# Turning the trunk by transposes of 64 rows instead of 128 in a two-layer hybrid decoder

## The chip, the cores and the metric

The kernel runs on one core of a Trainium2 chip. The metric is the device time in microseconds (us) of one execution, everything from the first load to the last store included. Times in this text are of the kernel before unless said otherwise.

Engines: PE multiplies matrices and transposes (PEld is its loading of weights, which overlaps), ScalarE (ACT), VectorE (DVE) and GpSimd (POOL) compute elementwise, SP issues the transfers. PE writes to PSUM, memory of 128 partitions in eight banks of 512 fp32 columns; ACT and DVE read it there.

## What is computed

Two layers of a decoder on 256 tokens of 1024 numbers, all in fp32. Cut to what matters here:

```python
def rms_norm(x, g):
    y = x * lax.rsqrt(jnp.mean(x * x, axis=-1, keepdims=True) + RMS_EPS)
    return y * g

def swiglu(x, w_gate, w_up, w_down):
    return (jax.nn.silu(x @ w_gate) * (x @ w_up)) @ w_down

h = x
for l in range(2):
    h = h + 0.5 * swiglu(rms_norm(h, ffn1_norm[l]), ...)      # 1024 -> 2816 -> 1024
    h = h + hybrid_mixer(rms_norm(h, mix_norm[l]), w_in[l], ...)  # three groups of attention heads
    h = h + 0.5 * swiglu(rms_norm(h, ffn2_norm[l]), ...)
```

So there are six stages (FFN, mixer, FFN in each layer), and at each of the five borders between them the trunk `h` has to be normed and turned, so that features lie on partitions for the matmuls that follow.

## The kernel before

**Precision.** A product in fp32 is made of three in a faster format: each operand is split into a high part (rounded) and a low part (the rest). A weight block of 128 x 1024 is loaded by SP, its high part `wh` is cast by ACT (L126) and its low part `wl` subtracted by DVE (L130). These splits run ahead of PE through the whole kernel, up to seven blocks.

**The trunk at a border.** `trunk` holds 256 tokens (two tiles `t` of 128 partitions) by 1024 features. The class `Norm` makes of it `xhl`: for each of eight blocks `m` of 128 features the turned 128 x 256 tokens, times the gain, as a high part (`high`, L364, on ACT) and a low part (`low`, L367, on DVE; it subtracts the high part from the product, and so reads both). Both read the turned block out of PSUM. The division by the root mean square comes later, out of sums of squares (`squares`, L390, on ACT; then L395, L350 on DVE).

**Halves.** A border is done in two halves of four blocks, `half(0)` and `half(1)`. `turn` (L370 to L376) puts the eight 128 x 128 transposes of a half into two banks of tag `acc`, two blocks `m` to a bank. Four high parts, four low parts and the squares follow.

**Where the halves stand.** Instructions stand on each engine in the order in which the code issues them; nothing reorders them. At the end of a FFN (`tail`, L659) the trunk is finished in four quarters `q` of 128 tokens x 512 features, each by 12 matmuls and a residual add on DVE (L419). `half(0)` stands behind quarter 2's residual, ahead of quarter 3's on DVE, while PE goes on with quarter 3's matmuls. `half(1)` needs the last residual; it stands in the next stage: in a mixer inside `index_queries` (L762) after the first two column groups of the first unit, in a FFN behind the first eight wide matmuls (L594). Behind a mixer the first half is taken apart: its transposes are `norm_T`, its parts `norm_out` (L1289 to L1300), which stands some matmuls later.

Of the ten halves, four are at the entry of the two mixers, four behind the two mixers, two between the layers. The border at the very start (`opening`) has transposes of its own and is not touched.

**After `half(1)` in a mixer.** DVE goes on with weight splits, the sum of squares and then L781, which takes the finished index queries out of the four `gu` banks. PE's next chunk of `w_in` goes into those banks.

**The helper that exists.** `turn(ps, i, src)` at module level (L177 to L180) transposes a block in two halves of 64 rows, one into each of two banks: out of rows 0 to 63 come 64 columns in the first bank, out of rows 64 to 127 in the second. Attention uses it already for its probabilities, keys and gates.

Of the kernel before, what the change touches and what calls it, by code (L numbers as in the profile page):

```python
# [10 lines left out]
F32 = mybir.dt.float32  # L11
F32R = mybir.dt.float32r
I32 = mybir.dt.int32
AF = mybir.ActivationFunctionType
ALU = mybir.AluOpType
# [3 lines left out]
P = 128  # L19
# [135 lines left out]
def kernel(ctx: ExitStack, tc: tile.TileContext, x, ffn1_norm, ffn1_w_gate, ffn1_w_up, ffn1_w_down,  # L155
# [16 lines left out]
    V, A, G, T = nc.vector, nc.scalar, nc.gpsimd, nc.tensor  # L172

    def bank(tag):
        return psum.tile([P, 512], F32, name="ps_" + tag, tag=tag)

    def turn(ps, i, src):  # L177
        for e, b in enumerate(ps):
            r = slice(64 * e, 64 * e + 64)
            T.transpose(b[:, 64 * i:64 * i + 64], src[r], ident[r, r])  # L180
# [21 lines left out]
    trunk = xp.tile([P, 2, D], F32, name="trunk")  # L202
    cst = cp.tile([P, 3 * P + 2 * LATE], F32, name="cst")
    ident = cp.tile([P, P], F32, name="ident")
    rows, more_rows = tmp(P)[:16], tmp(P)[:32]
    gT = cp.tile([P, 48], F32, name="gT")
# [33 lines left out]
    def add_ffn(wg, wu, wd, first=False):  # L240
# [24 lines left out]
        for f in range(NF):  # L265
            half("g", f)
            half("u", f)
            if f == NF - 1:
                half("d", f - 1 - DOWN_LAG)
            if DOWN_LAG <= f != NF - 2:  # L270
                half("d", f - DOWN_LAG)
# [82 lines left out]
    class Norm:  # L354
# [5 lines left out]
            self.h, self.l = self.x[:, :, 0], self.x[:, :, 1]  # L360
            self.ss = sm.tile([P, 4], F32, name="ss4", tag="ss4")

        def high(self, m, src):
            A.activation(self.h[:, m], src, AF.Copy, scale=gT[:, self.col + m:self.col + m + 1])  # L364

        def low(self, m, src):
            V.scalar_tensor_tensor(self.l[:, m], src, gT[:, self.col + m:self.col + m + 1],  # L367
                                   self.h[:, m].bitcast(F32), op0=ALU.mult, op1=ALU.subtract)

        def turn(self, mp):  # L370

            ps = bank("acc").rearrange("p (m s) -> p m s", m=2)
            for t in range(2):
                for i in range(2):
                    T.transpose(ps[:, i, t * P:(t + 1) * P], trunk[:, t, (2 * mp + i) * P:(2 * mp + i + 1) * P], ident)  # L375
            return ps  # L376

        def half(self, c):

            ps = [self.turn(2 * c + i) for i in range(2)]  # L380
            srcs = [(4 * c + i, ps[i // 2][:, i % 2]) for i in range(4)]
            for m, src in srcs:
                self.high(m, src)
            for m, src in srcs:
                self.low(m, src)
            for t in range(2):
                self.squares(t, c)

# [34 lines left out]
    def ffn(norm, nxt, aside=None, first=False):  # L423
# [86 lines left out]
        def opening():  # L510
# [5 lines left out]
            def split(i, m, high, E):  # L516

                src, h, l = low[i]
                ks = slice(2 * m, 2 * m + 2)
                high(h[:, ks], src[:, ks])  # L520
                E.tensor_tensor(l[:, ks], src[:, ks], h[:, ks].bitcast(F32), op=ALU.subtract)  # L521
# [24 lines left out]
            def squares(c):  # L546
                for t in range(2):
                    norm.squares(t, c)

            xT = turn(0)  # L550
            warm_up(BRIDGE)
            for m in range(2):
                ks = (2 * m, 2 * m + 1)
                parts(m, xT)
                split(0, m, G.tensor_copy, V)
                split(1, m, A.copy, G)
                for k in ks:
                    wide(0, k)
                if m:
                    xT = turn(2)  # L560
                for k in ks:
                    narrow(0, k)
                if m:
                    squares(0)
                    parts(2, xT)
                xT = turn(2 * m + 1)
                for k in ks:
                    wide(1, k)
                for k in ks:
                    narrow(1, k)  # L570
# [11 lines left out]
            for f, p in enumerate((p0, p1)):  # L582
                for w, u in zip(p.ws, high):
                    for part, v in zip(w, u):
                        part.extend(v[:, k, f * P:(f + 1) * P] for k in range(4))
# [104 lines left out]
    def mixer(l, norm, nxt):  # L690
# [113 lines left out]
        def post_ib(ps):  # L804
# [113 lines left out]
            def sums_in():  # L918
                low, high = (at.tile([P, 4, 2, P], F32, name="later" + k, tag=k) for k in ("kT", "later"))
                first = tab.rearrange("p a b t d -> p (a b t d)").rearrange("p (h c) -> p h c", c=P)  # L920
                st["later"], st["first"] = (low, high), first
                src = sums_of
                for dst, h, n in ((first, 0, P), (low, 0, S), (high, 4, S)):
                    to = dst.rearrange("p h b c -> p h (b c)") if n == S else dst
                    k = to.shape[1]
                    nc.sync.dma_start(to, bass.AP(tensor=src.tensor, offset=src.offset + h * S,
                                                    ap=[[0, P], [S, k], [1, n]]))
# [119 lines left out]
        def tanh():  # L1047
            ps, hr = st.pop("cg"), st["hr"]
            sg = at.tile([P, 2, 512], F32, name="sg", tag="sg")
            for t in range(2):  # L1050
                A.activation(sg[:, t], ps[t], AF.Tanh, scale=hr[:, t:t + 1])
            st["sg"] = sg
# [139 lines left out]
        def both_scores(_):  # L1192
            for fn in (scores, st["B"][0]):
                for p in range(2):
# [4 lines left out]
                    b=lambda p: st["B"][1](p), B=lambda p: st["B"][2](p), T=lambda _: tanh(), w=causal_part)  # L1199
# [11 lines left out]
        for name, cols in CHUNKS[1:]:  # L1211
            n = sum(c[1] for c in cols)
            ps = [bank("gu") for _ in range(2)]
# [18 lines left out]
        acc = [bank("acc") for _ in range(4)]  # L1232
        late_sb = xp.tile([P, 3, 4, S], F32, name="cT", tag="xhl")
        st["gate"] = late_sb[:, 2]
        after = {}
# [51 lines left out]
            after["norm"] = nxt()  # L1287

        def norm_T(_):  # L1289
            after["ps"] = [after["norm"].turn(i) for i in range(2)]  # L1290

        def norm_out(_):
            n, ps = after["norm"], after["ps"]
            for m in range(4):
                n.high(m, ps[m // 2][:, m % 2])
            for m in range(4):
                n.low(m, ps[m // 2][:, m % 2])
            for t in range(2):
                n.squares(t, 0)

        todo.update(f=lambda p: flip(p, acc[2:]), c=c_T, k=c_out, g=gate_T, l=gate_out, h=left, r=right, x=last_right,
                    p=lambda _: W.pump(), Z=residuals, N=norm_T, M=norm_out)
        do(AC_ORDER)
        W.pump()
# [3 lines left out]
    def before_mixer(l):  # L1308
        if l == 0:
            V.memset(causal[:, P:2 * P], 0.0)  # L1310
            for t in range(2):
                V.tensor_scalar(causal[:, 2 * t * P:(2 * t + 1) * P], future, NEG, None, op0=ALU.mult)
            V.tensor_tensor(gc[:, 0], gc[:, 0], gc[:, 1], op=ALU.mult)
            V.tensor_scalar(gc[:, 0], gc[:, 0], HD ** -0.5, None, op0=ALU.mult)
        mixer_tables(l)
# [8 lines left out]
    norm = Norm(0, 0)  # L1324
    turn_gains()
    for l in range(DEPTH):
        norm = ffn(norm, lambda: Norm(1, l), lambda: before_mixer(l), l == 0)
        norm = mixer(l, norm, lambda: Norm(2, l))
        norm = ffn(norm, (lambda: Norm(0, l + 1)) if l + 1 < DEPTH else None)
# [37 lines left out]
```

## Time and profile before

| | us |
|---|---|
| median of 3 runs | 1005.16 |
| lowest, highest | 1004.29, 1005.18 |
| the profiled execution | 1004.51 |
| its span from the first instruction to the last | 1002.8 |

| engine | busy, share of the span | instructions |
|---|---|---|
| PE | 100% | 5692 |
| DVE | 80% | 1484 |
| ACT | 60% | 1118 |
| POOL | 16% | 186 |

1.7 us of the profiled execution lie outside its span. In a timeline a row of "x8" is eight like instructions in a row: its start is that of the first, its duration reaches to the end of the last. Instructions of an engine overlap a little, so the next row can start before the one ahead has ended. What stands in brackets is the idle time of the engine before the row and what it waited for; an idle time is given only where the engine's last instruction had ended.

### The profile page before, as it was taken

The numbers are of one execution on the slowest core, as the hardware profiler recorded it, in microseconds if no ns is written. First come the engines' busy times: TensorE is split into PE (matmuls) and PEld (weight loads), VectorE is DVE, ScalarE is ACT, GpSimd is POOL, SyncE is SP. The second block draws the span as 40 slices with busy tenths as digits, with TensorE's granted clock in tenths as the row PEclk, the third lists the DMA queues.
The fourth block names the chain that finished last, engine by engine and source line by source line (L and its number), as shares of the span: only waits on it lengthen the run. The fifth ranks groups of instructions, "written<-read, shape, count | busy, mean of one in ns | idle before, by whom it ended". The sixth has DMA issues, their size and how long they took to land.

```text
span 1002.8 us, 15209 instructions
## 1 busy us (share of the span) xinstructions
PE 998.1 (100%) x5692; PEld 856.6 (85%) x5692; DVE 797.5 (80%) x1484; ACT 598.2 (60%) x1118; POOL 160.9 (16%) x186
## 2 busy tenths in 40 slices
PE   9999999999999999999999999999999999999998
PEld 8888888888878888888888888889888788888887
DVE  5977778789998777777888777787899877777776
ACT  6655555587776555555465555556868765555552
POOL 2002000057902000000000030001677110000000
PEclk9999999999999999999999999999999999999999
DMA  9865746475725555555655655565556255474731
GB/s 293 270 223 160 231 149 238 140 245 172 241 72 168 167 169 185 193 190 202 196 168 173 210 184 195 193 200 184 181 202 231 83 175 165 135 242 144 235 127 42
DMA packets 133498, 184.80 MB, mean 184 GB/s; under 512 B 7152, under 2 KB 106800, under 8 KB 133424
## 3 DMA queue, kind: packets, MB, share of 16 engines
q1 hardware_dynamic: 133392, 183.82, 56.1%
q8 instruction: 45, 0.74, 0.3%
q14 instruction: 29, 0.24, 0.1%
q10 hardware_dynamic: 32, 0.01, 0.0%
HBM read 182.75 MB, written 1.06 MB: 183 GB/s over the span
## 4 chain that ended last, share of the span: by engine, by line
PE 88%; DVE 9%; ACT 2%; issue 1%; POOL 0%; DVEq 0%; ACTq 0%; POOLq 0%
PE ps_gu L340 57%; PE ps_acc L340 29%; DVE wl L130 4%; DVE score L889 1%; PE ps_acc L375 1%; ACT p L1095 1%; DVE score L875 1%; DVE m L888 1%; DVE c_ss L728 0%; PE ps_acc L180 0%; PE ps_gu L180 0%; DVE tmp L1085 0%; DVE p L1113 0%; DVE xhl L367 0%; DVE amask L893 0%
## 5 line engine op out<-in xcount | busy, mean ns | idle before, releaser
L130 DVE TENSOR_TENSOR wl<-raw,wh 128x1024 fp32r<-128x1024 f32 (+2 forms) x342 | 418.6, 1232 | 28.8 <-ACT wh L126 28.8
L126 ACT CAST wh<-raw 128x1024 fp32r<-128x1024 f32 (+2 forms) x341 | 341.7, 1037 | 15.2 <-PE ps_acc L340 8.2
L340 PE MATMUL ps_gu<-xhl,wh 128*128 128x512 f32 (+1 forms) x1472 | 347.6, 388 | 0.0
L340 PEld LDWEIGHTS ps_gu<-xhl,wh 128*128 128x128 f32 x1472 | 272.6, 188 | 54.2 <-ACT wh L126 0.5
L340 PEld LDWEIGHTS ps_gu<-xhl,wl 128*128 128x128 f32 x1472 | 187.5, 191 | 4.1 <-DVE wl L521 0.2
L340 PE MATMUL ps_gu<-xhl,wl 128*128 128x256 f32 (+1 forms) x1472 | 190.3, 282 | 0.0
L484 DVE TENSOR_TENSOR tmp<-ps_gu,tmp 128x256 f32<-128x256 f32 x176 | 72.9, 423 | 109.6 <-ACT tmp L483 109.3
L340 PE MATMUL ps_acc<-wh,hh 128*128 128x512 f32 (+1 forms) x352 | 137.2, 390 | 0.0
L340 PE MATMUL ps_acc<-wl,hh 128*128 128x512 f32 (+1 forms) x352 | 137.1, 389 | 0.0
L340 PE MATMUL ps_acc<-wh,hl 128*128 128x512 f32 (+1 forms) x352 | 136.6, 388 | 0.0
L340 PE MATMUL ps_gu<-wh,xhl 128*128 128x512 f32 (+2 forms) x448 | 134.6, 376 | 0.1
L483 ACT COPY tmp<-ps_gu 128x256 f32<-128x256 f32 x176 | 63.5, 372 | 91.6 <-PE ps_gu L340 91.4
L498 ACT CAST hh<-tmp 128x256 fp32r<-128x256 f32 x80 | 32.6, 407 | 120.3 <-DVE tmp L495 120.3
L340 PEld LDWEIGHTS ps_gu<-wh,xhl 128*128 128x128 f32 x448 | 82.6, 188 | 14.7 <-issue 1.7
L490 ACT ACTIVATE tmp<-tmp 128x256 f32<-128x256 f32 x88 | 36.9, 419 | 83.3 <-DVE tmp L488 83.2
L340 PE MATMUL ps_gu<-wl,xhl 128*128 128x512 f32 (+2 forms) x224 | 83.2, 372 | 0.0
L340 PEld LDWEIGHTS ps_acc<-wh,hl 128*128 128x128 f32 x352 | 66.1, 188 | 13.8
L351 POOL TENSOR_TENSOR y_n<-msq,minus_half 128x2 f32<-128x2 f32 x6 | 7.0, 1175 | 440.2 <-DVE msq L350 440.2
L340 PEld LDWEIGHTS ps_acc<-wh,hh 128*128 128x128 f32 x352 | 66.3, 188 | 12.6
L340 PEld LDWEIGHTS ps_acc<-wl,hh 128*128 128x128 f32 x352 | 66.3, 188 | 12.4 <-DVE wl L130 0.2
L340 PEld LDWEIGHTS ps_gu<-wl,xhl 128*128 128x128 f32 x224 | 42.1, 188 | 5.7
L508 DVE TENSOR_TENSOR tmp<-tmp,rb 128x256 f32<-128x256 f32 x88 | 37.5, 427 | 3.0
(232 smaller groups left out, 902.4 us busy)
## 6 DMA issues: line engine op xcount, KB each, us to landing
raw<-in_ffn_w_down_dram SPq DMA_DIRECT2D x44, 1024.0 KB, 5.0
raw<-in_ffn_w_gate_dram SPq DMA_DIRECT2D x42, 1024.0 KB, 7.3
raw<-in_ffn_w_up_dram SPq DMA_DIRECT2D x42, 1024.0 KB, 8.1
raw<-in_w_in_dram SPq DMA_DIRECT2D x24, 1024.0 KB, 5.1
raw<-in_w_out_dram SPq DMA_DIRECT2D x8, 1024.0 KB, 5.0
raw<-in_w_in_dram SPq DMA_DIRECT2D x4, 768.0 KB, 4.6
raw<-in_w_in_dram SPq DMA_DIRECT2D x4, 656.0 KB, 4.1
raw<-in_ffn_w_gate_dram SPq DMA_DIRECT2D x3, 512.0 KB, 7.4
```

The lines of the kernel that those rows point to most:

```text
L126: self.nc.scalar.copy(hv, src)
L130: (engine or self.nc.vector).tensor_tensor(lv, self.srcs[self.n_low], hv.bitcast(F32), op=ALU.subtract)
L340: T.matmul(o, l, r, start=start, stop=stop, skip_group_check=True)
L375: T.transpose(ps[:, i, t * P:(t + 1) * P], trunk[:, t, (2 * mp + i) * P:(2 * mp + i + 1) * P], ident)
L483: A.copy(o, ps[:, 1])
L484: V.tensor_tensor(o, ps[:, 0], o, op=ALU.add)
L490: A.activation(th, t_, AF.Tanh, scale=0.5)
L498: (V.tensor_copy if late else A.copy)(hh, t_)
L508: V.tensor_tensor(t_, t_, norm.rb, op=ALU.mult)
L875: V.scalar_tensor_tensor(sc, rl[e][:, i * n:(i + 1) * n], st["iw"][:, t, h:h + 1], st["cmask"][t] if h == 0 else sc, op0=ALU.mult, op1=ALU ...
L888: V.max(out=m8, in_=st["score"][t])
L889: V.match_replace(out=st["score"][t], in_to_replace=m8, in_values=st["score"][t], imm_value=-3e38)
```

## The change

Each of the eight transposes of 128 rows in a half becomes two of 64 rows by the helper. All four blocks `m` of a half now lie in both banks: one bank holds the tokens that came from rows 0 to 63 of each tile (64 for each `t`), the other those from rows 64 to 127. The high and the low part of a block are each taken in two pieces of 128 columns, one out of each bank (`e` = 0 and 1), and written to two runs of 64 columns of `xhl`. The order in a half is: all transposes, all eight high pieces, all eight low pieces, the squares.

```diff
-        def high(self, m, src):
-            A.activation(self.h[:, m], src, AF.Copy, scale=gT[:, self.col + m:self.col + m + 1])
+        def place(self, x, m, e):
+            x = x[:, m]
+            return x if e is None else x.rearrange("p (t j) -> p t j", t=2)[..., 64 * e:64 * e + 64]
+
+        def high(self, m, src, e=None):
+            A.activation(self.place(self.h, m, e), src, AF.Copy, scale=gT[:, self.col + m:self.col + m + 1])
...
-            ps = bank("acc").rearrange("p (m s) -> p m s", m=2)
-            for t in range(2):
-                for i in range(2):
-                    T.transpose(ps[:, i, t * P:(t + 1) * P], trunk[:, t, (2 * mp + i) * P:(2 * mp + i + 1) * P], ident)
-            return ps
+        def turns(self, c):
+
+            ps = [bank("acc") for _ in range(2)]
+            for m in range(4):
+                for t in range(2):
+                    turn(ps, 2 * m + t, trunk[:, t, (4 * c + m) * P:(4 * c + m + 1) * P])
+            return [b.rearrange("p (m t j) -> p m t j", t=2, j=64) for b in ps]
+
+        def parts(self, c, ps):
+
+            for f in (self.high, self.low):
+                for m in range(4):
+                    for e in range(2):
+                        f(4 * c + m, ps[e][:, m], e)
 
         def half(self, c):
 
-            ps = [self.turn(2 * c + i) for i in range(2)]
-            srcs = [(4 * c + i, ps[i // 2][:, i % 2]) for i in range(4)]
-            for m, src in srcs:
-                self.high(m, src)
-            for m, src in srcs:
-                self.low(m, src)
+            self.parts(c, self.turns(c))
...
         def norm_T(_):
-            after["ps"] = [after["norm"].turn(i) for i in range(2)]
+            after["ps"] = after["norm"].turns(0)
```

Line numbers below `Norm` move by 4 to 6: L364 becomes L368, L367 L371, L419 L425, L781 L787.

On DVE at the entry of the first mixer there stand, before, three residuals, the four low parts of the first half, the last residual, a weight split and the four low parts of the second half. A name in brackets is the engine whose counter the instruction waits for:

```order
L419 SCALAR_TENSOR_TENSOR trunk<-ps_acc,trunk 128x512 [waits PE_49] x3
L367 SCALAR_TENSOR_TENSOR xhl<-ps_acc,gT,xhl 128x256 [waits PE_49,Activation_49]
L367 SCALAR_TENSOR_TENSOR xhl<-ps_acc,gT,xhl 128x256
L367 SCALAR_TENSOR_TENSOR xhl<-ps_acc,gT,xhl 128x256 [waits PE_49,Activation_49]
L367 SCALAR_TENSOR_TENSOR xhl<-ps_acc,gT,xhl 128x256
L419 SCALAR_TENSOR_TENSOR trunk<-ps_acc,trunk 128x512 [waits PE_49]
L130 TENSOR_TENSOR wl<-raw,wh 128x1024 [waits DMAHW1_49]
```

And on DVE at the same place after the change:

```order
L425 SCALAR_TENSOR_TENSOR trunk<-ps_acc,trunk 128x512 [waits PE_49] x3
L371 SCALAR_TENSOR_TENSOR xhl<-ps_acc,gT,xhl 128x2x64 [waits PE_49,Activation_49] x2
L371 SCALAR_TENSOR_TENSOR xhl<-ps_acc,gT,xhl 128x2x64 x6
L425 SCALAR_TENSOR_TENSOR trunk<-ps_acc,trunk 128x512 [waits PE_49]
L130 TENSOR_TENSOR wl<-raw,wh 128x1024 [waits DMAHW1_49]
```

There are eight low parts where there were four, and the two that wait for ACT are the first and the second: the first of each bank.

On PE, at the second half in the same mixer, before (`xhl` with `wh` are the index queries):

```order
L340 MATMUL ps_gu<-xhl,wl 128x192 x2
L375 MATMUL ps_acc<-ident,trunk 128x128 x2
L375 MATMUL ps_acc<-ident,trunk 128x128 [waits DVE_49]
L375 MATMUL ps_acc<-ident,trunk 128x128
L375 MATMUL ps_acc<-ident,trunk 128x128 [waits PE_49]
L375 MATMUL ps_acc<-ident,trunk 128x128 x3
```

On PE at the same place after the change:

```order
L340 MATMUL ps_gu<-xhl,wl 128x192 x2
L180 MATMUL ps_acc<-ident,trunk 128x64
L180 MATMUL ps_acc<-ident,trunk 128x64 [waits DVE_49,PE_49]
L180 MATMUL ps_acc<-ident,trunk 128x64 [waits DVE_49]
L180 MATMUL ps_acc<-ident,trunk 128x64 x13
```

Of sixteen transposes the second already writes the other bank, and the third reads the tile `t` = 1, which the last residual on DVE finishes.

## Rows read from the trace of the kernel before

**Rows 1.** The page: busy time of each engine; granted clock in 40 slices.

```profile
PE 998.1 (100%) x5692; PEld 856.6 (85%) x5692; DVE 797.5 (80%) x1484; ACT 598.2 (60%) x1118; POOL 160.9 (16%) x186
...
PEclk9999999999999999999999999999999999999999
```

**Rows 2.** Timeline, PE, first mixer's first half: start us, us, engine, line, operation, count.

```profile
187.70 0.39 PE L340 MATMUL ps_acc<-wh,hl 128*128 128x512 f32 x1
187.93 1.03 PE L375 MATMUL ps_acc<-ident,trunk 128*128 128x128 f32 x8
...
189.03 0.40 PE L340 MATMUL ps_acc<-wl,hh 128*128 128x512 f32 x1
```

**Rows 3.** Timeline, PE, two blocks of 64-row transposes in the first layer's attention.

```profile
264.70 0.39 PE L340 MATMUL ps_gu<-wh,xhl 128*128 128x512 f32 x1
265.02 0.96 PE L180 MATMUL ps_acc<-ident,p 64*128 64x64 f32 x24
...
266.25 0.40 PE L340 MATMUL ps_gu<-wl,xhl 128*128 128x512 f32 x1
...
289.61 0.72 PE L180 MATMUL ps_acc<-ident,sg 64*128 64x64 f32 x16
```

**Rows 4.** Groups by line and shape: out<-in, count, busy us, mean ns, idle us before.

```profile
L364 ACT ACTIVATE xhl<-ps_acc,gT 128x256 fp32r<-128x256 f32 x48 | 19.1, 475 | 30.2 <-PE ps_acc L375 27.0 <-PE ps_acc L537 3.2
...
L739 ACT ACTIVATE bqr<-ps_gu,y_n 128x256 f32<-128x256 f32 x4 | 2.0, 498 | 0.0
...
L739 ACT ACTIVATE vA<-ps_gu,y_n 128x64 f32<-128x64 f32 x4 | 1.3, 331 | 0.0
...
L367 DVE SCALAR_TENSOR_TENSOR xhl<-ps_acc,gT,xhl 128x256 fp32r<-128x256 f32 x48 | 20.1, 478 | 10.1 <-ACT xhl L364 10.1
...
L1085 DVE CUSTOM_DVE_ANT_0 tmp<-ps_gu,tab 128x128 f32<-128x128 f32 x16 | 4.6, 288 | 1.0 <-PE ps_gu L340 1.0
...
L1085 DVE CUSTOM_DVE_ANT_0 tmp<-ps_gu,laterkT 128x256 f32<-128x256 f32 x8 | 3.4, 420 | 0.0
```

**Rows 5.** Timelines of ACT and DVE, first mixer's entry, and DVE's busy time 195 to 201.

```profile
188.56 1.57 ACT L364 ACTIVATE xhl<-ps_acc,gT 128x256 fp32r<-128x256 f32 x4 [6.99 <-PE ps_acc L375]
...
189.44 1.66 DVE L367 SCALAR_TENSOR_TENSOR xhl<-ps_acc,gT,xhl 128x256 fp32r<-128x256 f32 x4 [0.62 <-ACT xhl L364]
191.74 0.69 DVE L419 SCALAR_TENSOR_TENSOR trunk<-ps_acc,trunk 128x512 f32<-128x512 f32 x1 [0.64 <-PE ps_acc L340]
...
194.17 1.66 DVE L367 SCALAR_TENSOR_TENSOR xhl<-ps_acc,gT,xhl 128x256 fp32r<-128x256 f32 x4 [0.61 <-ACT xhl L364]
...
195.00:201.00 6.00, 5.96 (x11) 1.00 0.48 147
...
201.36 0.88 DVE L781 TENSOR_TENSOR iqr<-ps_gu,tmp 128x192 f32<-128x192 f32 x3
```

**Rows 6.** PE's loading of weights behind the index queries; two rows of the waits (us, times, longest).

```profile
201.75 0.19 PEld L340 LDWEIGHTS ps_gu<-wh,xhl 128*128 128x128 f32 x1 [0.23 <-DVE iqr L781]
...
PEld ps_acc L854 <- DVE ikd L818: 0.7, 2, 0.4
...
PEld ps_gu L340 <- DVE iqr L781: 0.5, 2, 0.2
```

**Rows 7.** Timelines between the layers: low parts; PE's wide matmuls on each half.

```profile
501.72 1.66 DVE L367 SCALAR_TENSOR_TENSOR xhl<-ps_acc,gT,xhl 128x256 fp32r<-128x256 f32 x4 [0.62 <-ACT xhl L364]
...
503.82 1.98 PE L340 MATMUL ps_gu<-xhl,wh 128*128 128x512 f32 x8
...
510.26 2.00 PE L340 MATMUL ps_gu<-xhl,wh 128*128 128x512 f32 x8
```

**Rows 8.** Timelines behind the first mixer: low parts, last residual, second transposes.

```profile
316.26 1.66 DVE L367 SCALAR_TENSOR_TENSOR xhl<-ps_acc,gT,xhl 128x256 fp32r<-128x256 f32 x4 [1.35 <-ACT xhl L364]
...
319.88 0.69 DVE L419 SCALAR_TENSOR_TENSOR trunk<-ps_acc,trunk 128x512 f32<-128x512 f32 x1 [0.21 <-PE ps_acc L340]
...
321.50 1.03 PE L375 MATMUL ps_acc<-ident,trunk 128*128 128x128 f32 x8
```

More of the change, by code (lines that the diff above doesn't have):

```diff
@@ L361, in __init__, with low @@
             self.ss = sm.tile([P, 4], F32, name="ss4", tag="ss4")
-        def high(self, m, src):
-            A.activation(self.h[:, m], src, AF.Copy, scale=gT[:, self.col + m:self.col + m + 1])
[L366 to L370, printed above, removed]
-            ps = bank("acc").rearrange("p (m s) -> p m s", m=2)
-            for t in range(2):
-                for i in range(2):
-                    T.transpose(ps[:, i, t * P:(t + 1) * P], trunk[:, t, (2 * mp + i) * P:(2 * mp + i + 1) * P], ident)
-            return ps
-        def half(self, c):
-            ps = [self.turn(2 * c + i) for i in range(2)]
-            srcs = [(4 * c + i, ps[i // 2][:, i % 2]) for i in range(4)]
-            for m, src in srcs:
-                self.high(m, src)
-            for m, src in srcs:
-                self.low(m, src)
+        def place(self, x, m, e):
[3 more added lines that the diff above has]
+            A.activation(self.place(self.h, m, e), src, AF.Copy, scale=gT[:, self.col + m:self.col + m + 1])
+        def low(self, m, src, e=None):
+            V.scalar_tensor_tensor(self.place(self.l, m, e), src, gT[:, self.col + m:self.col + m + 1],
+                                   self.place(self.h, m, e).bitcast(F32), op0=ALU.mult, op1=ALU.subtract)
+        def turns(self, c):
[9 more added lines that the diff above has]
+                        f(4 * c + m, ps[e][:, m], e)
+        def half(self, c):
+            self.parts(c, self.turns(c))
             for t in range(2):
@@ L1289, in norm_T @@
         def norm_T(_):
-            after["ps"] = [after["norm"].turn(i) for i in range(2)]
+            after["ps"] = after["norm"].turns(0)
         def norm_out(_):
[L1293 to L1297, printed above, removed]
+            n = after["norm"]
+            n.parts(0, after["ps"])
             for t in range(2):
```

## The prediction

> **What bounds the kernel now.** I read the page first. TensorE is busy for 998.1 of 1002.8 us [rows 1], so time is won only by taking work from PE, and lost wherever PE is made to wait. ScalarE (60%) and VectorE (80%) have room on average; the question is whether they have it at the borders. The granted clock is full in all 40 slices [rows 1]. Then I read PE's timeline around a block of trunk transposes and around blocks of 64-row transposes that the kernel already has [rows 2, 3], for the price on PE; the groups of ACT and DVE that read PSUM, for the price of a piece [rows 4]; their timelines at the entry of the first mixer [rows 5], behind which PE's loading of weights already waits 0.23 us for DVE [rows 6]; and the two other kinds of border [rows 7, 8].
>
> **PE's own price.** There are ten blocks of eight 128-row transposes. With the one at 187.93 in place, 1.33 us lie between the starts of the last wide matmul before it and of the second one behind it, at 189.03 [rows 2]. The block of 24 64-row transposes takes 1.55 us between the same two marks, 264.70 to 266.25 [rows 3]. 24 of them take 0.96 us and 16 take 0.72, so four pairs are 0.24 and a pair (the two halves of one 128-row transpose) is 0.06 us [rows 3]. Sixteen then take 1.55 - 0.24 = 1.31 us between the marks: 0.02 less than now, 0.04 at most by rounding. The steps are short, but the way in is longer: 0.32 us from the last wide matmul to the first transpose, against 0.23 [rows 2, 3]. Ten blocks give 0.2 to 0.4 us.
>
> [...]
>
> **Price on ScalarE and VectorE.** Four high parts of 256 columns take 1.57 us and one takes 0.475, so each further one adds 0.365 [rows 4, 5]. Eight of 128 columns replace them. That form is not in the trace. Two other activations of L739 out of PSUM take 331 ns with 64 columns and 498 with 256: 0.17 us for 192 columns, 0.113 for 128 [rows 4]. So a high part takes 0.362 and each further one adds 0.252. A low part takes 0.478, a further one adds 0.394 ((1.66 - 0.478) / 3); DVE's operation of L1085 on PSUM takes 288 ns with 128 columns and 420 with 256, 0.132 less [rows 4, 5]. That gives 0.346 and 0.262. The ends are half (0.18 and 0.20), as if columns were all, and no saving (0.365 and 0.394). I take the interpolations, since either is between two rows of the same engine reading PSUM. By them eight pieces cost ACT and DVE 0.5 us more than four did.
>
> **The wait that moves.** The first low part starts at 189.44 after 0.62 us of idling on ACT [rows 5]. The first high part was over at 188.56 + 0.475 = 189.04, the second at 189.40. So a low part waits for the last high part that reads its *bank*, not for its own. Now a bank holds two of the four column blocks. After the change each bank holds 64 rows' worth of all four, and the high parts go round both: the first low part waits for the seventh of eight, the second for the eighth, and the first high part for the fifteenth of sixteen transposes. In the order the two waits stand at the first two low parts, which fits, and the new transposes and pieces stand where the diff says; that it does nothing is no case.
>
> [...]
>
> **Mixer entry, twice, step by step** [rows 2 to 6]; the time before stands in brackets. The first transpose starts at 187.70 + 0.32 = 188.02 and the sixteenth is done 0.72 later, at 188.74. The first high part starts 0.04 behind it, at 188.78 [188.56]. The seventh ends 6 x 0.252 + 0.362 = 1.87 later, at 190.65, and the first low part starts at 190.69 [189.44]. Eight of them hold DVE for 8 x 0.262 = 2.10, to 192.79. Behind them on DVE stands the residual of the trunk's last quarter, which started at 191.74 as soon as PE had finished; now it starts at 192.79 and ends at 193.48. The second block of transposes reads what it writes: its third transpose starts at 193.54 and makes PE wait. Seven pairs (0.43) and the last's own 0.22 later the banks are full, near 194.14; the high parts start at 194.18, the seventh ends at 196.05, the low parts start at 196.09 [194.17] and end 7 x 0.262 + 0.346 later, at 198.27 [195.83]: DVE is 2.44 us late. From 195 to 201 DVE is busy for 5.96 of 6.00 us, up to the first L781 at 201.36 [rows 5], so nothing is made up. PE's first matmul of the next chunk of `w_in` needs the bank that this L781 empties: its loading of weights waits for it at 201.75 [rows 6], and goes to 204.19. **+2.44 us**, and the waits have this pair twice [rows 6]: +4.9. A little comes back: PE waits 0.7 us in two places for the turned index key (L854) [rows 6], which is on DVE and would now be there first or no later. Between 0 and 0.35 each, I take 0.2: -0.4.
>
> **The other borders.** Between the layers the first low part moves by the same 1.25 us, from 501.72 to 502.97, and the last ends 2.18 later, at 505.15. PE's eight wide matmuls there start at 503.82 at 0.227 us each ((1.98 - 0.39) / 7, a matmul's own row being 0.39); the fourth wants the fourth block at 504.50 [rows 2, 7], and that comes at 505.21: **+0.7**. The second half is wanted only at 510.26 [rows 7], behind sixteen more matmuls. Its low parts, 1.25 + 0.52 us later and behind a residual that moves with PE, still end before that; I cost them at nothing, and at the same 0.7 if that cover fell short.
>
> Behind each mixer the high parts stand behind a cast on ACT and start as before, so the first low part moves by 1.87 - 0.84 = 1.03, from 316.26 to 317.29, and the last one ends 0.52 more late, 1.55 in all. The last residual, at 319.88, had 0.21 to spare [rows 8], and the 0.08 by which a row of DVE can start ahead of the last one's end (0.478 against 0.394); so it is 1.26 late and ends at 321.83, and the third transpose, due at 321.50 + 0.2 = 321.70, starts at 321.89. That is +0.2, of which PE's gain takes back 0.04: twice +0.15, **+0.3**.
>
> **Sum.** 4.9 - 0.4 + 0.7 + 0.3, less 0.2 for PE's gain at the six blocks where it is not in the above: **+5.3 us**. Against the profiled execution (1004.51) that is 1009.8. The median of three runs is 0.65 above it, so by that it would be 1010.5; I write 1010.1, between the two. Each 0.01 us on a high part's step moves a mixer by 2 x 0.06, on a low part's by 2 x 0.08; 0.03 on both is 0.84 a mixer, 1.7 in all. With 0.7 either way for the covers the forecast's own range is 1007.5 to 1012.5. The ends of the two prices lie further out: with halves a mixer loses 12 x 0.072 + 16 x 0.062 = 1.9 less, with no saving 12 x 0.113 + 16 x 0.132 = 3.5 more, 1006.1 and 1016.8 in all; the upper one would need 128 columns to cost ACT and DVE what 256 do, which the two pairs of [rows 4] that differ in columns speak against.
>
> **Rivals.**
> A, no change: the low parts follow their own high part, not the bank's last. Then the first starts near 189.18 and DVE is free at 191.3, before the residual; only some 0.3 us of the second half's added work on DVE reaches PE, in two mixers, less PE's 0.2 to 0.4: +0.2 to +0.4, 1004.7 to 1005.5. Against it speaks the idle of 0.62 us, for it that DVE has room on average. 8%.
> B, faster: 64-row transposes take half the time, and DVE's delay finds cover that I don't see. A block costs 1.33 - 2 x 0.227 = 0.88 us beyond the two matmuls, half is 0.44, ten are 4.4: 1000.1. [Rows 3] speak against it. 3%.
> [...] 9%.
> D, the sum: 80%.
>
> **How the numbers follow.** D is the likeliest. The range of 1006.5 to 1013.0 takes in D's own with a margin on both sides and leaves out most of A, B and C, 2 in 10. 0.2%, some 2 us, is about what a measurement of this kernel can tell from no change. B and a little of A make 4% for faster, the rest of A 8% for no change with the low edge of D, and 88% are left for slower.
>
> **What would show it.** In the profile after: the first low part of a block idles about 1.9 us on ACT, not 0.62; PE's loading of weights waits about 2 us for L787 (now L781) twice; PE waits for the last residual (L425) in the second block of each mixer entry, and for low parts near 504.5 between the layers; sixteen transposes show about 0.72 us. I am wrong if low parts start after their own high part, if 128 columns cost far from 0.25 us a step, or if DVE's queue between 195 and 201 has slack that its busy time doesn't show.

## The result: slower by 9 us, just outside the range

| | before | after |
|---|---|---|
| median of 5 runs, us | 1004.88 | 1013.92 |
| lowest, highest | 1004.29, 1005.18 | 1012.47, 1014.12 |
| profiled execution, its span | 1004.51, 1002.8 | 1012.47, 1010.8 |
| mean granted clock, profiled | 1.000 | 0.998 |

The ratio is 1.0088, with a 95% interval of 1.0077 to 1.0099. Slower was forecast, and by the steps that were forecast; the size was not: 1013.92 against 1010.1 and a range up to 1013.0.

The page of the profile after, busy times and counts, beside [rows 1]:

```profile
PE 1001.2 (99%) x5772; PEld 855.2 (85%) x5772; DVE 801.5 (79%) x1524; ACT 603.8 (60%) x1158; POOL 160.9 (16%) x186
```

80 more instructions on PE, 40 on DVE and on ACT. No engine has become the bound by its work; what has grown most is the time in which PE waits (span less busy time: 4.7 us before, 9.6 after).

**The first mixer's entry.** Timelines of PE, ACT and DVE in the profile after (start, us, engine, line, operation, count, idle before); they answer to [rows 2, 5, 6]:

```profile
187.90 0.39 PE L340 MATMUL ps_acc<-wh,hl 128*128 128x512 f32 x1
188.22 0.71 PE L180 MATMUL ps_acc<-ident,trunk 64*128 64x64 f32 x16
...
189.20 0.39 PE L340 MATMUL ps_acc<-wl,hh 128*128 128x512 f32 x1
...
193.31 1.07 PE L180 MATMUL ps_acc<-ident,trunk 64*128 64x64 f32 x16
...
204.46 0.42 PE L340 MATMUL ps_gu<-wh,xhl 128*128 128x336 f32 x1 [1.88 <-DVE iqr L787]
```

```profile
188.97 2.18 ACT L368 ACTIVATE xhl<-ps_acc,gT 128x128 fp32r<-128x128 f32 x8 [7.20 <-PE ps_acc L180]
```

```profile
190.92 2.16 DVE L371 SCALAR_TENSOR_TENSOR xhl<-ps_acc,gT,xhl 128x128 fp32r<-128x128 f32 x8 [1.90 <-ACT xhl L368]
193.00 0.68 DVE L425 SCALAR_TENSOR_TENSOR trunk<-ps_acc,trunk 128x512 f32<-128x512 f32 x1
...
196.37 2.16 DVE L371 SCALAR_TENSOR_TENSOR xhl<-ps_acc,gT,xhl 128x128 fp32r<-128x128 f32 x8 [1.56 <-ACT xhl L368]
```

Everything in this execution stands 0.21 us later from the first 14 us on, before any border. Less that, the forecast chain is there link by link: high parts from 188.76 (forecast 188.78), low parts from 190.71 (190.69) after 1.90 us of idling, the residual at 192.79 (192.79), the second low parts at 196.16 (196.09), PE's next chunk at 204.25 (204.19). Mark to mark a block of transposes takes 187.90 to 189.20, 1.30 us (forecast 1.31, before 1.33).

**Where the 8.0 us of span come from.** Read as the shift of the same matmul of PE between the two traces, ahead of and behind each place:

| place | forecast | measured |
|---|---|---|
| the opening, before any border | 0 | +0.21 |
| entry of the first mixer | +2.44 | +2.49 |
| its turned index key, later | -0.2 | -0.23 |
| behind the first mixer | +0.15 | +0.16 |
| between the layers | +0.7 | +0.83 |
| entry of the second mixer | +2.44 | +2.56 |
| **granted clock behind it** | 0 | **+1.46** |
| its turned index key | -0.2 | -0.18 |
| behind the second mixer | +0.15 | +0.19 |
| within the attentions | 0 | +0.14, +0.33 |
| PE's gain elsewhere | -0.2 | not seen by itself |
| sum | +5.3 | +7.96 |

The row that isn't in the sum is the clock. The windows of the profile after, around PE's standstill in the second mixer (window; its length; busy us and instructions of PE, PEld, DVE, ACT, POOL; granted clock; DMA share; GB/s):

```profile
702.00:703.00 1.00, 0.44 (x4) 0.27 (x2) 1.00 (x3) 1.00 (x6) 0.00 (x0) 1.00 1.03 389
703.00:704.00 1.00, 0.00 (x0) 0.00 (x0) 1.00 (x2) 1.00 (x2) 0.00 (x0) 1.00 0.95 292
704.00:705.00 1.00, 0.69 (x4) 0.69 (x5) 1.00 (x5) 0.03 (x1) 0.66 (x2) 0.89 1.04 346
705.00:706.00 1.00, 1.00 (x5) 1.00 (x4) 1.00 (x2) 0.98 (x3) 1.00 (x2) 0.50 0.97 255
706.00:707.00 1.00, 1.00 (x5) 1.00 (x5) 1.00 (x2) 0.95 (x4) 1.00 (x2) 0.50 0.88 292
707.00:708.00 1.00, 1.00 (x5) 1.00 (x4) 1.00 (x3) 0.95 (x4) 0.69 (x2) 0.50 1.04 403
708.00:709.00 1.00, 1.00 (x7) 1.00 (x7) 1.00 (x4) 0.97 (x2) 0.00 (x0) 0.90 1.07 395
```

PE stands still from 702.4 to 704.3. Some 0.5 us after its going on the granted clock falls from 1.00 to 0.50 (0.89 is the mean of the window from 704 to 705), and it stays there for 3.4 us, to 708.2. The matmuls of that stretch, then those behind it:

```profile
705.22 0.48 PE L340 MATMUL ps_gu<-wl,xhl 128*128 128x336 f32 x1
705.50 0.76 PE L340 MATMUL ps_gu<-wh,xhl 128*128 128x336 f32 x2
706.06 0.48 PE L340 MATMUL ps_gu<-wl,xhl 128*128 128x336 f32 x1
...
708.42 0.32 PE L340 MATMUL ps_gu<-wl,xhl 128*128 128x336 f32 x1
708.57 0.47 PE L340 MATMUL ps_gu<-wh,xhl 128*128 128x336 f32 x2
708.88 0.32 PE L340 MATMUL ps_gu<-wl,xhl 128*128 128x336 f32 x1
```

Three matmuls take 0.84 us (705.22 to 706.06) at a granted clock of 0.50 and 0.46 (708.42 to 708.88) at 1.00. In the first mixer of the same execution, behind a standstill of 1.88 us (here 1.87), the clock stayed at 1.00. The other four runs have a mean clock of 0.996 or 0.997 and spans of 1012.2 to 1012.5, 1.4 to 1.7 above the profiled 1010.8: what a second fall would add.

### The profile page after: what moved, and what is told of

It is laid out like the page before. It is cut to its first block, busy times and chain, and to the rows that moved or that the text cites. A ratio compares the mean times of both kernels' runs of the same rounds, so it can differ in the third digit from the quotient of the medians.

```text
span 1010.8 us, 15459 instructions
## 1 busy us (share of the span) xinstructions
PE 1001.2 (99%) x5772; PEld 855.2 (85%) x5772; DVE 801.5 (79%) x1524; ACT 603.8 (60%) x1158; POOL 160.9 (16%) x186
## 4 chain that ended last, share of the span: by engine, by line
PE 92%; DVE 3%; ACT 2%; DMA 1%; issue 0%; SPq 0%; DVEq 0%; ACTq 0%
PE ps_gu L340 62%; PE ps_acc L340 29%; DVE wl L130 2%; PE ps_acc L180 1%; DMA raw<-in_ffn_w_up_dram 1%; ACT xhl L368 1%; ACT wh L126 1%; ACT p L1101 0%; DVE xhl L371 0%; PE ps_gu L180 0%; DVE p L1119 0%; SPq L100 0%; ACT tmp L396 0%; DVE score L895 0%; SPq L225 0%
## 5 line engine op out<-in xcount | busy, mean ns | idle before, releaser
L368 ACT ACTIVATE xhl<-ps_acc,gT 128x128 fp32r<-128x128 f32 (+1 forms) x88 | 25.2, 392 | 30.7 <-PE ps_acc L180 27.7
```

The lines of the kernel that those rows point to most:

```text
L368: A.activation(self.place(self.h, m, e), src, AF.Copy, scale=gT[:, self.col + m:self.col + m + 1])
```

## Experiments

Times are medians; the kernel before, run beside them on the same chips, had 1004.81 (first four, and e7 to e11), 1004.71 (the next four) and 1004.94 (e12, e13).

### What carries the loss: the wait, the pieces or the transposes

**e1, the order of the pieces alone.** One bank after the other instead of by turns:

```diff
             for f in (self.high, self.low):
-                for m in range(4):
-                    for e in range(2):
+                for e in range(2):
+                    for m in range(4):
                         f(4 * c + m, ps[e][:, m], e)
```

> The changed kernel with its pieces in another order: the four high parts out of one bank, then the four out of the other, and the low parts the same. Nothing else differs, so the number and size of all instructions are those of the changed kernel. Theory W (a low part waits for the last high part that reads its bank): the first low part waits for the fourth high part instead of the seventh, 3 x 0.26 = 0.78 us less idle (1.90 to about 1.1) in every block; two blocks one behind the other give the mixer entry 1.5 us back, PE's wait for L787 goes from 1.88 to about 0.9, and the rest of the loss with it: 1006.4, and if the clock falls only behind the long wait, it stays up. Rival P (the pieces' own fixed costs on ACT and DVE hold the queue, the wait is beside the point): the same number of pieces, so no change, 1012 to 1014.

Measured: 1006.73, ratio 1.0019 (1.001 to 1.0029), clock 0.999 to 1.000. DVE's timeline at the first mixer and PE's wait at L787 (us, times, longest):

```profile
190.36 2.16 DVE L371 SCALAR_TENSOR_TENSOR xhl<-ps_acc,gT,xhl 128x128 fp32r<-128x128 f32 x8 [1.12 <-ACT xhl L368]
```

```profile
PE ps_gu L340 <- DVE iqr L787: 2.2, 2, 1.1
```

The same instructions in another order give back 7.2 of 9.0 us, some 3 of them by the clock. The idle falls by the 0.78 that three high parts take: the wait goes by the bank.

**e2, the wait alone,** in the kernel before:

```diff
-            srcs = [(4 * c + i, ps[i // 2][:, i % 2]) for i in range(4)]
+            srcs = [(4 * c + i, ps[i % 2][:, i // 2]) for i in range(4)]
```

(and the transposes to match).

> The kernel before with its four blocks dealt to the two banks by turns (first and third in one, second and fourth in the other); transposes of 128 rows, pieces of 256 columns, all in the same order and number. Theory W: the first low part waits for the third high part instead of the second, 0.365 us later; idle of 0.62 becomes about 0.98 in every block, DVE ends 0.37 later at L781, PE +0.3 in each mixer: about 1005.4 (+0.5). Rival P, and the rival of the prediction in which a low part waits for its own high part: idle stays 0.62, time stays 1004.9.

Measured: 1005.76, ratio 1.0011 (1.0001 to 1.002). DVE's timeline:

```profile
190.16 1.66 DVE L367 SCALAR_TENSOR_TENSOR xhl<-ps_acc,gT,xhl 128x256 fp32r<-128x256 f32 x4 [1.05 <-ACT xhl L364]
```

Idle of 1.05 where [rows 5] have 0.62. Only the place of the blocks has changed, so a wait for a part's own high part (rival A) is out.

**e3, the pieces alone,** with transposes and banks of before:

```diff
+        def parts(self, srcs):
+
+            for x in (self.h, self.l):
+                for m, src in srcs:
+                    for t in range(2):
...
-            for m, src in srcs:
-                self.high(m, src)
-            for m, src in srcs:
-                self.low(m, src)
+            self.parts(srcs)
```

> The kernel before with its transposes and banks, but every high and low part in two pieces of 128 columns (one for each tile of tokens), in the order all high, all low. Isolates the price of eight pieces instead of four, with the wait nearly as it was: the first low part now waits for the fourth of eight. Theory W: idle 3 x 0.26 + 0.36 = about 1.1 us less the start, +0.3; DVE 0.5 longer; L781 is 0.8 to 0.9 later in each mixer: 1006.2 (+1.3), clock up. Rival P: all of the changed kernel's loss is here too, 1010 to 1014.

Measured: 1006.24, ratio 1.0014 (1.0004 to 1.0023). DVE's timeline:

```profile
190.05 2.16 DVE L387 SCALAR_TENSOR_TENSOR xhl<-ps_acc,gT,xhl 128x128 fp32r<-128x128 f32 x8 [0.92 <-ACT xhl L385]
```

Eight pieces instead of four, with the short wait, cost 1.4 us. e1 (64 rows) and e3 (128 rows) have the same pieces and a first low part behind the fourth high part, and differ by 0.5.

**e4, the transposes alone.** 64-row transposes, parts of 256 columns out of each bank as before:

```diff
-            ps = [self.turn(2 * c + i) for i in range(2)]
+            ps = self.turns(c)
```

> The kernel before with the 64-row transposes of the changed kernel, but parts of 256 columns, two out of each bank as before; the columns that are read are not those of the block that is named, so the output is not the reference's, while the number, size, order and waits of all instructions on ACT and DVE are those of before. Isolates what the transposes themselves cost. My sum: 0.02 to 0.04 us less on PE for each of ten blocks, high parts 0.2 us later, so 1004.9 within 0.4. Rival B of the prediction (64 rows take half the time): 1000.5. Rival T (the transposes of 64 rows are what slows the changed kernel, by themselves or by a lower clock): 1007 or more, clock below 1.0.

Measured: 1004.33, ratio 0.9996 (0.9986 to 1.0005): no change that can be told. PE's timeline around the first block:

```profile
187.66 0.39 PE L340 MATMUL ps_acc<-wh,hl 128*128 128x512 f32 x1
187.98 0.71 PE L180 MATMUL ps_acc<-ident,trunk 64*128 64x64 f32 x16
188.62 0.50 PE L340 MATMUL ps_acc<-wh,hh 128*128 128x512 f32 x1
188.96 0.39 PE L340 MATMUL ps_acc<-wl,hh 128*128 128x512 f32 x1
```

Mark to mark 187.66 to 188.96, 1.30 us again: 0.03 for each of ten blocks. Half the price (rival B) is out. ACT and DVE have here the pieces and the order of before, so this is about all that the transposes can bring: 0.5 us by the medians, 1.4 at most by the interval.

**e6, the change at the six other borders alone:**

```diff
+            if self.col in (16, 24):
+                ps = [self.turn(2 * c + i) for i in range(2)]
...
+            else:
+                self.parts(c, self.turns(c))
```

> The change made at the six other blocks alone (two between the layers, four behind the mixers); the four at the mixers' entry as before. My sum: 0.7 between the layers and 0.3 behind the mixers, +0.8 to +1.2: 1005.9, clock up; the changed kernel's other 8 us then lie at the mixers' entry. Rival: the loss is spread evenly over the ten blocks, 0.9 each: 1010.

Measured: 1005.92, ratio 1.0011 (1.0002 to 1.0021), clock 1.000. So 1.2 us lie there, and the other 7.8, with the falls of the clock, at the mixers' entry.

### What brings the clock down

**The changed kernel once more.**

> The changed kernel once more, for a second trace and the clock of each run. Theory C (behind a standstill of PE of 1.9 us the granted clock can fall to the lower level, in each of the two mixers on its own): runs differ by steps of about 1.5 us with the mean clock, 1010.9 with no fall (clock 1.000), 1012.4 with one (0.998), 1013.9 with two (0.997 or 0.996). Rival: the time differs without the clock.

Measured: 1014.15, 1012.40 to 1014.41. Here the profile was of a run at 1014.41, and the windows show the clock at 0.50 behind both mixers' standstills (1.87 and 1.86 us):

```profile
206.00:207.00 1.00, 1.00 (x5) 1.00 (x5) 1.00 (x1) 0.95 (x4) 1.00 (x2) 0.50 0.73 202
...
709.00:710.00 1.00, 1.00 (x5) 1.00 (x5) 1.00 (x3) 0.95 (x4) 0.63 (x1) 0.50 1.03 385
```

The runs fall on two of the three steps expected: one at 1012.40 with a mean clock of 0.998, three at 1014.11 to 1014.41 with 0.997. Read so, the clock fell behind 16 of the 18 standstills of the changed kernel's nine runs; its time without a fall would be near 1010.9 (no run of it had none).

**e5 and e7, a standstill without the change.** The kernel before with unused sums on DVE ahead of the first L781 of each mixer:

```diff
+                    if u == 3 and f == 0:
+                        for _ in range(2):
+                            V.tensor_reduce(idle, trunk[:, :, :512], axis=AX.X, op=ALU.add)
                     if u == 3:
                         o = tmp(LATE)
```

(two of 1024 numbers in e5_delay_long, where they took 2.47 us together, one in e5_delay_short, one of 1024 and one of 512 in e7_delay_middle).

> The kernel before with two sums of 128 x 1024 numbers on DVE (about 1.07 us each, their result used by nobody) ahead of the first L781 of each mixer: a standstill of PE as long as the changed kernel's, without its transposes and pieces. Theory C: PE waits about 2.2 us for DVE at L781 in each mixer, the time is 1008.9 with the clock up and 1.5 more for each mixer behind which it falls, 1010.4 or 1011.8, mean clock 0.998 or 0.997. Rival T (the fall comes from the 64-row transposes or the small pieces): 1008.9 in every run, clock 1.000.

> The same with one sum, a standstill of about 1.1 us. Theory C: clock stays up, +0.9 in each mixer, 1006.8. If a wait of any length brings it down: 1008.3 to 1009.8 and a clock below 1.000.

> The kernel before with two unused sums on DVE ahead of the first L781 of each mixer (1024 and 512 numbers in a row), so that PE stands still for about 1.9 us there, as long as in the changed kernel (1.88), without its transposes and pieces. +1.75 in each mixer less 0.2: 1008.0 with the clock up, and 1.5 to 1.9 more for each mixer behind which it falls. Theory C1 (the length of the standstill decides alone): falls in nearly all runs as in the changed kernel, 1011 to 1011.5 and a mean clock of 0.997. Rival C2 (the standstill is needed, but how often the clock falls behind it hangs on something else too): falls in some runs or none, clock 0.998 to 1.000, 1008 to 1010.

PE's wait for that line (us, times, longest) in the long, the short and the middle one:

```profile
PE ps_gu L340 <- DVE iqr L784: 4.9, 2, 2.4
```

```profile
PE ps_gu L340 <- DVE iqr L784: 2.4, 2, 1.2
```

```profile
PE ps_gu L340 <- DVE iqr L784: 3.8, 2, 1.9
```

Measured: the long one 1010.16, in two pairs (1009.12 and 1009.30 at a clock of 1.000, 1011.03 and 1011.23 at 0.998); the short one 1007.30, 1.000 in all nine runs; the middle one 1008.39 (1007.68 to 1008.39 at 1.000 in three, 1009.78 and 1010.05 at 0.998 in two). So a standstill alone brings the clock down in some runs, with none of the change in the kernel, for 1.8 to 1.9 us by the means of the runs; C2 holds against C1. The longer standstill (2.4 us) did it in 2 of 8 passes, the one of the changed kernel's length (1.9) in 2 of 10.

**e8, the same delay with the 64-row transposes** (e4 with the sums of e7).

> The same delay in the kernel with the 64-row transposes and parts of 256 columns out of the wrong columns (so its output is not the reference's). Differs from the run before by the transposes alone. 1007.6 with the clock up. If the 64-row transposes make the fall more likely (rival T): falls in most runs here and in few of the run before. Theory C1 or C2 without the transposes: as often as in the run before, within what a few runs can tell.

Measured: 1010.00 (1008.22 to 1011.32): no fall in one run, one in two, two in two, 6 of 10 passes. PE's wait is a little longer than in e7:

```profile
PE ps_gu L340 <- DVE iqr L792: 4.3, 2, 2.1
```

More falls than in e7, but five runs of each are too few to tell 6 of 10 from 2 of 10. So the question was put the other way round as well.

**e12, everything of the change but its transposes.** Blocks by turns as in e2, pieces as in e3, in an order in which the first low part waits for the seventh high part:

```diff
+            for x in (self.h, self.l):
+                for t in range(2):
+                    for m, src in srcs:
...
+            srcs = [(4 * c + i, ps[i % 2][:, i // 2]) for i in range(4)]
+            self.parts(srcs)
```

> Everything of the change but its transposes: transposes of 128 rows, blocks dealt to the two banks by turns, eight high and eight low parts of 128 columns in an order in which the first low part waits for the seventh high part, as in the changed kernel. Theory W: the first low part idles about 1.9 us, DVE is some 2.0 us late at L781, PE stands still for 1.5 to 1.8 us there in each mixer: 1009.7 with the clock up, 1.5 more for each fall. Rival T (the 64-row transposes make the fall frequent): clock 1.000 in most runs, 1009.5 to 1010. Against T (waits on DVE's queue make it frequent): one or two falls in most runs, clock 0.998 or 0.997, 1011.2 to 1012.7.

DVE's timeline at the first mixer, and PE's wait:

```profile
190.96 2.16 DVE L388 SCALAR_TENSOR_TENSOR xhl<-ps_acc,gT,xhl 128x128 fp32r<-128x128 f32 x8 [1.88 <-ACT xhl L386]
```

```profile
PE ps_gu L340 <- DVE iqr L791: 3.3, 2, 1.7
```

Measured: 1012.64, ratio 1.007 (1.0056 to 1.0084): two runs at 1011.06 and 1011.24 with the clock at 1.000, three at 1012.64 to 1012.77 with 0.998. With the clock up, e12 is as slow as the changed kernel would be (near 1010.9): wait and pieces are enough for the whole loss, without 64-row transposes. It is not the changed kernel in every wait: PE waits for ACT's L400 three times, 1.6 us in all and 0.5 at the longest, which it doesn't there. The 1009.7 expected was 1.4 too low; the residual ahead of the second half is late here too (193.03), and by the shift of PE's matmuls the borders between the layers and behind the mixers cost as much as in the changed kernel (0.8, and 0.2 each). The clock falls without 64-row transposes, in 3 of 10 passes.

**e13, the transposes and pieces with a short wait, and a delay.** e1 with one sum of 640 numbers.

> The changed kernel with its pieces in the order of banks, and one unused sum of 640 numbers in a row on DVE ahead of the first L787, so that PE's standstill is again near 1.9 us though the wait of the first low part is the short one. With the clock up 1008.2. If the standstill brings the clock down whatever makes it long: some runs 1.5 or 3.0 above that with clocks of 0.998 and 0.997. Rival T: most runs, since the 64-row transposes are there. If neither: 1008.2 in all runs, clock 1.000.

PE's wait:

```profile
PE ps_gu L340 <- DVE iqr L789: 3.6, 2, 1.8
```

Measured: 1008.98; three runs at 1008.26 to 1008.98 (clock 1.000), one at 1010.26 (0.998), one at 1011.51 (0.997): 3 of 10 passes, though the 64-row transposes are all there. That is as often as in e12 without them, and speaks against rival T as far as five runs can.

Together, by the mean clock of each run (0.998 is one fall, as in the traces of the changed kernel and of e10; 0.997 is two, as in that of after_again; 0.996, in a single run of the changed kernel, is read as two; a pass is one mixer in one run). The last two rows are of e10 and e11, told below, where PE waits twice, with one transpose between:

| PE's wait in a mixer, us | kernels | passes with a fall |
|---|---|---|
| 0.2 to 1.2 | e1, e2, e3, e4, e5 short | 0 of 98 |
| 1.7 to 1.8 | e12, e13 | 6 of 20 |
| 1.9 | changed kernel | 16 of 18 |
| 1.9 | e7 | 2 of 10 |
| 2.1 | e8 | 6 of 10 |
| 2.4 | e5 long | 2 of 8 |
| 1.1 and 0.6 | e10 | 4 of 8 |
| 1.4 and 0.6 | e11 | 0 of 10 |

No fall behind a single short wait, falls in some passes behind each of the long ones. The length doesn't decide alone: 2.4 us did it less often than the changed kernel's 1.9, and e11's pair not at all, though it is longer than e10's. Why the changed kernel has falls in nearly every pass, and standstills about as long in a third, is **open**: neither its transposes (e13) nor its waits on DVE (e12) bring it about alone. Nor does the chip: on one and the same, after_again had 7 of 8 and e5 long 2 of 8.

One rival is left that no experiment tested: the moment at which the standstill comes. By the windows of after, after_again and e10, PE had gone on for 0.5 to 1.2 us when the clock fell, in four falls. Of the changed kernel's two standstills in the first mixer, both 1.9 us long, the one behind which the clock stayed up began at 202.58 (first trace), the other at 202.97 (after_again). Whether those 0.4 us matter was not shown. Each experiment moved its standstill in time too, so the counts don't separate an edit from its timing.

### Can the delay be kept from PE

**e10 and e11, two weight splits moved behind L787,** in the changed kernel and in the one before:

```diff
                 run_side()
-                W.pump(2)
+                if u != 2:
+                    W.pump(2 if u < 3 else 4)
```

> The changed kernel, with the two weight splits that the third unit of the index queries issues put behind L787 of the fourth (four there instead of two). Nothing else moves. If the loss at a mixer's entry is carried to PE by DVE's queue in front of L787 (my sum), some 1.9 us of splits leave that queue: PE's wait for L787 goes from 1.88 to 0 to 0.3, the standstill and with it the fall of the clock are gone, and about 0.7 a mixer (the late second block of transposes) and 1.2 at the other borders stay: 1007.2, clock 1.000. If PE needs those splits at once, or ACT's queue holds L787 as well: 1009 or more.

> The same move in the kernel before, to see if it beats it: the wait of PE's loading of weights (0.23 us in each mixer) would go, and the 0.06 that it costs PE: 1004.4 to 1004.8, no change that can be told. If PE needs the two splits earlier: 1005.5 to 1006.5.

Measured: 1013.13 (ratio 1.0083, 1.0069 to 1.0096) and 1008.57 (1.0038, 1.0024 to 1.0051), both far off. PE's waits of more than 1 us for DVE in the changed kernel with the move, and in the kernel before with it:

```profile
PE ps_acc L861 <- DVE ikd L825: 3.5, 4, 1.1
```

```profile
PE ps_acc L855 <- DVE ikd L819: 3.9, 4, 1.4
```

The wait at L787 is gone, and the turned index key, for which PE waits in two places in the kernel before, 0.7 us together [rows 6], is now late in four. The splits were not in the way, they were in their place: the move costs 3.8 us by itself (e11). So e10 doesn't show what the loss would be without DVE's queue at L787; it shows that lateness of DVE, taken out of one wait, came out at the next. In e10 the clock fell once in each of four runs (0.998), in the profiled one behind these two waits, with PE idle for 1.14 and 0.61 us and one transpose between:

```profile
717.14 0.33 PE L861 MATMUL ps_acc<-ident,ikd 128*128 128x128 f32 x1 [1.14 <-DVE ikd L825]
718.09 0.33 PE L861 MATMUL ps_acc<-ident,ikd 128*128 128x128 f32 x1 [0.61 <-DVE ikd L825]
```

No version that beats the kernel before came out of this; e4 puts what there was to win at some 0.5 us, 1.4 at most.

## Why the prediction was wrong

**PE's own price: right.** 1.31 us forecast, 1.30 in the changed kernel and in e4; e4 alone gains 0.5 us, within its noise the 0.2 to 0.4 forecast. Rival B is refuted: half the time was a guess that no run shows, and these blocks went from 1.33 to 1.30.

**Price of the pieces: right.** Eight high parts took 2.18 us, eight low parts 2.16; with 0.383 and 0.342 for one (groups of the profile after) a further one adds 0.257 and 0.260, against 0.252 and 0.262 forecast:

```profile
L368 ACT ACTIVATE xhl<-ps_acc,gT 128x128 fp32r<-128x128 f32 x80 | 21.8, 383 | 27.7 <-PE ps_acc L180 27.7
L371 DVE SCALAR_TENSOR_TENSOR xhl<-ps_acc,gT,xhl 128x128 fp32r<-128x128 f32 x80 | 21.6, 342 | 15.8 <-ACT xhl L368 15.8
```

**The wait that moves: right.** Idle of 1.90 us against 0.62, and by experiment: e2 lengthens it by the place of the blocks alone, e1 shortens it by the order alone. Rival A is refuted. One step of the working is added up wrongly: 193.54 + 0.43 + 0.22 is 194.19, not 194.14, and most of the 0.07 by which the second low parts came late is there.

**The borders: nearly right.** The two entries together 5.05 against 4.9, between the layers 0.83 against 0.7, behind the mixers 0.35 against 0.3. e6 measured the six blocks outside the mixers at 1.2 against the 0.8 to 1.2 expected of it. The sum without the clock comes to about 1010.9 in the runs (1012.4 less 1.5), inside the forecast's own range.

**The step that failed is the chance of a lower clock: the sum put its fall at nothing.** I had it among the rivals: C, at 9%, was that PE stands still for some 2 us in one piece in each mixer entry and that its granted clock falls behind it, 1014. That it would fall was my guess, since no row of before has such a standstill or a lower clock; so none showed that the clock would stay up either. The sum itself made a standstill of that length certain in both mixers. Given that, C's chance was the chance that the clock falls behind 1.9 us, of which I knew nothing, and 9% was far too sure. It fell in 16 of 18. C's price was too high: it took +4 for the two mixers, which no run shows, and a fall cost 1.46 in the profiled run and 1.4 to 1.9 in the runs. With C's fall at the measured price the sum is 1010.9 + 2 x 1.5 = 1013.9, which is the median. That C's own figure, 1014, hits it too is luck: its sum was 0.8 too low and its price 1.0 too high. The range stopped at 1013.0 because it left C out.

## What to carry to other kernels

In these kernels a reader of PSUM on DVE waited for the last one on ACT in the same bank (e1, e2), so the order of the readers is part of the layout: when blocks are spread over two banks, take one bank whole before the other (here 7.2 us for two swapped lines). Work that an in-order engine gets late reached PE at the end of its queue in full, since the queue had no gaps (DVE busy for 5.96 of 6.00 us [rows 5]): DVE was 2.44 us late by the forecast, and PE lost 2.49 and 2.56. A forecast that makes PE of such a kernel stand still for about 2 us has to price a fall of its clock as a likely case, not as a mishap: here it came in 16 of 18 passes of the changed kernel and in 2 of 10 to 6 of 10 of the experiments at 1.7 to 2.4 us, and cost 1.4 to 1.9 us each.

## What was not expected of the hardware

The granted clock can fall behind standstills of PE of 1.7 to 2.4 us, within the span of a kernel that keeps PE busy for 99%, and whether it does differs from run to run of one and the same program (e5 long, e7, e12, e13); behind single waits of up to 1.2 us it never did in 98 passes, behind two of 1.1 and 0.6 us it did in 4 of 8 (e10). In the four falls read by windows (after, after_again twice, e10) the clock falls to 0.50 when PE has gone on for 0.5 to 1.2 us, not while it stands, and holds there for 3.4 us. A fall cost 1.4 to 1.9.
